# Making the output product's first 1024 columns in pairs of row blocks by pairs of column blocks, two of them with seven products

## The chip, the cores and the metric

The kernel runs on one core of one Trainium2 chip. The metric is the time of one execution on the device, in microseconds (us); smaller is better. Three executions of the kernel before took 1020.9, 1021.13 and 1021.59 us, so the median is 1021.13 us. PE is TensorE (matrix multiplication), DVE is VectorE, ACT is ScalarE, POOL is GpSimd and SP is SyncE, which here only issues transfers.

## The reference, cut to what matters

The input is one sequence of 256 rows with 2048 features. After a normalisation and one wide projection, two mixers (attention and a short gated convolution) make `y_mla` and `y_conv`. They are merged by gates, the merged rows go through one more 2048 by 2048 product, and the result is normalised and added to the input:

```
merged = jax.nn.sigmoid(g_mla) * y_mla + jax.nn.sigmoid(g_conv) * y_conv
out = jnp.einsum('bsd,de->bse', merged, w_out)
x = x + _rmsnorm(out, post_norm_g)
```

The change concerns `out`, that is `merged` (256 x 2048) times `w_out` (2048 x 2048), and what stands around it in the program.

## The kernel before

**Numbers in two parts.** Every operand of a product is a float32 array that is written as a sum of two arrays of TensorE's faster format, a high part and a low part. ACT copies an array to its high part, and DVE takes the difference as its low part (`split_act`, lines L287 and L288). One logical product is then three matmuls: high by high, high by low, low by high (`product`; all matmuls have line L90). One matmul has a 128 x 128 stationary operand (a piece of the activations, turned so that features lie on partitions) and 512 moving columns (a piece of a weight matrix).

**Weight units.** Weights come from HBM in units of 128 x 2048 numbers, 1 MB each, in the fixed order of the list `plan`. `take(i)` is called where unit i is used. It first calls `ahead(i)`, which issues the transfers of the units up to i + 2 (from SP, into one of three `raw` buffers) and the split of unit i + 1. A plain unit is split as two halves of 1024 columns, each into a buffer of the ring `whi` (high) and one of the ring `wlo` (low). Both rings have five buffers, so a new half waits until the buffer freed longest ago has been read by its last matmul. A `raw` buffer comes free when the last split that reads it is done. A scheduler then sets the order of instructions on each engine, but keeps matmuls in the order of the code; each engine runs its own list strictly in order.

**Seven products.** The four 2048 x 2048 products ahead of the output product are made in blocks of two row blocks by two column blocks: a weight unit holds, for one pair of k blocks, four 128 x 512 weight blocks. A plain pair takes 8 products (24 matmuls). Some pairs are done with seven products (21 matmuls), as in Winograd's form of Strassen's scheme: DVE makes four sums of weight blocks (`split_seven`, L229: `ts`), all of which are split as well (`th`, `tl`; the third block goes to `ph`, `pl`), and four differences of activation blocks (`mixed`, L670: `xm`, split into a `mix` tile). The seven results lie in seven PSUM banks, and DVE combines them at the block's end (`first_sums`, L1078). In these products all partial products of a kind are summed over the pairs in PSUM.

**The output product.** Its weights `wo` are 16 units: four column blocks of 512 by four groups of four k blocks. The list `out_order` (L158) sets their order: column blocks 0, 1, 2 with the first two k groups each, then column blocks 0, 1, 2 with the other two, then column block 3 with all four. Every unit takes 24 matmuls, 12 for each of the two row blocks. Six PSUM banks collect column blocks 0 to 2. The activations are `merged`, in the tile `x_both`; `features(c)` splits four k blocks of it, which the last part of the product before brings back from HBM turned (`turned`, L370, L378 and L382). `features(2)` and `features(3)` stand in the code at the sixth unit.

**Around it.** After the sixth unit the pool `spool` (sums, gates) and the stacks below it are closed, and ACT's queue issues the loads of `gb` (the gain, 1 MB) and `xr` (the input rows, 2 MB) into memory that comes free there (L1198, L1199). As each of column blocks 0 to 2 ends, `out_block` takes its squares on ACT (L1204) and multiplies by `gb` on DVE (L1207). The splits of the last column block go to buffers of their own in the pools `op` and `op_w`. The end of the program scales, adds `xr` and stores.

## Time and profile before

| | |
|---|---|
| times of three executions | 1020.9, 1021.13, 1021.59 us |
| the profiled execution's own time | 1021.97 us |
| its span in the profile | 1020.2 us |
| mean granted TensorE clock | 0.999 |
| PE busy | 1013.9 us of the span |
| DVE busy | 812.7 us of the span |
| ACT busy | 564.0 us of the span |
| read from HBM | 215.66 MB |

The span runs from the first to the last instruction that the profiler saw; the execution's own time is 1.77 us longer. A row of a timeline gives the start in the span, the duration, the engine, the source line, the operation, its output and its inputs; "x2" stands for two such instructions in a row, and a bracket for the idle time ahead of it and what ended it. Instructions of one engine overlap a little, so that the next one starts before the duration of the one before has passed.

### The profile page before, as it was taken

The numbers are of one execution on the slowest core, as the hardware profiler recorded it, in microseconds if no ns is written. First come the engines' busy times: TensorE is split into PE (matmuls) and PEld (weight loads), VectorE is DVE, ScalarE is ACT, GpSimd is POOL, SyncE is SP. The second block draws the span as 40 slices with busy tenths as digits, with TensorE's granted clock in tenths as the row PEclk, the third lists the DMA queues.
The fourth block names the chain that finished last, engine by engine and source line by source line (L and its number), as shares of the span: only waits on it lengthen the run. The fifth ranks groups of instructions, "written<-read, shape, count | busy, mean of one in ns | idle before, by whom it ended". The sixth has DMA issues, their size and how long they took to land.

```text
span 1020.2 us, 12873 instructions
## 1 busy us (share of the span) xinstructions
PE 1013.9 (99%) x4621; PEld 844.2 (83%) x4621; DVE 812.7 (80%) x1174; ACT 564.0 (55%) x793; POOL 178.9 (18%) x344
## 2 busy tenths in 40 slices
PE   9999999999999999999999999999999999999997
PEld 7888888888888888888888888888888888888886
DVE  7578777777777777777878799899989979898572
ACT  7665655555556455455554556565766545363551
POOL 4640421113311213212132220000000000123000
PEclk9999999999999999999999999999999999999999
DMA  9774776567675767757676765555546546586852
GB/s 343 282 271 186 259 237 234 204 219 257 219 273 185 243 232 242 271 186 239 222 253 236 267 243 208 209 209 202 206 171 243 191 180 216 172 313 217 332 195 83
DMA packets 44528, 233.27 MB, mean 229 GB/s; under 512 B 7952, under 2 KB 10512, under 8 KB 21552
## 3 DMA queue, kind: packets, MB, share of 16 engines
q1 hardware_dynamic: 32400, 199.67, 54.8%
q0 software_dynamic: 11632, 29.48, 8.8%
q10 hardware_dynamic: 432, 3.29, 0.8%
q8 instruction: 36, 0.59, 0.2%
q14 instruction: 28, 0.23, 0.1%
HBM read 215.66 MB, written 12.58 MB: 224 GB/s over the span
## 4 chain that ended last, share of the span: by engine, by line
PE 95%; DMA 3%; ACT 1%; DVE 0%; issue 0%; SPq 0%; DVEq 0%; ACTq 0%
PE cv L90 34%; PE q L90 18%; PE p L90 9%; PE out L90 9%; PE z L90 6%; PE d L90 6%; PE vv L90 2%; PE kn L90 2%; PE qa L90 2%; PE qn L90 2%; PE ckv L90 2%; PE sc L90 1%; PE qr L90 1%; PE o L90 1%; DMA raw<-wz_dram 1%; DMA at_f<-far_qa 1%
## 5 line engine op out<-in xcount | busy, mean ns | idle before, releaser
L287 ACT ACTIVATE whi<-raw 128x1024 fp32r<-128x1024 f32 (+1 forms) x351 | 356.3, 1032 | 323.4 <-PE cv L90 109.4
L288 DVE TENSOR_TENSOR wlo<-raw,whi 128x1024 fp32r<-128x1024 f32 (+1 forms) x349 | 412.1, 1191 | 132.5 <-ACT whi L287 125.2
L90 PE MATMUL cv<-whi,x_both 128*128 128x512 f32 x1024 | 319.8, 389 | 0.0
L90 PEld LDWEIGHTS cv<-whi,x_both 128*128 128x128 f32 x1024 | 192.3, 188 | 39.5
L90 PE MATMUL cv<-wlo,x_both 128*128 128x512 f32 x512 | 199.6, 390 | 0.0
L90 PEld LDWEIGHTS cv<-wlo,x_both 128*128 128x128 f32 x512 | 96.1, 188 | 19.5 <-DVE wlo L288 0.2
L90 PE MATMUL q<-whi,x_both 128*128 128x512 f32 x296 | 97.1, 389 | 0.0
L90 PE MATMUL z<-whi,x_both 128*128 128x512 f32 x256 | 80.0, 389 | 0.0
L90 PE MATMUL out<-whi,x_both 128*128 128x512 f32 x256 | 78.9, 389 | 0.0
L378 POOL DMA_DIRECT2D far<-g x32 | 17.4, 551 | 312.7 <-DVE g L370 310.0
L378 POOL DMA_DIRECT2D far<-via x64 | 35.2, 556 | 180.7 <-DVE via L370 180.7
L90 PE MATMUL p<-whi,x_both 128*128 128x512 f32 x186 | 66.4, 390 | 0.0
L90 PEld LDWEIGHTS q<-whi,x_both 128*128 128x128 f32 x296 | 55.6, 188 | 11.5
L90 PE MATMUL q<-wlo,x_both 128*128 128x512 f32 x148 | 57.6, 389 | 0.0
L90 PEld LDWEIGHTS out<-whi,x_both 128*128 128x128 f32 x256 | 48.0, 188 | 9.9
L90 PEld LDWEIGHTS z<-whi,x_both 128*128 128x128 f32 x256 | 48.1, 188 | 9.9
L287 ACT ACTIVATE th<-ts 128x1024 fp32r<-128x1024 f32 x42 | 44.3, 1054 | 19.8 <-DVE ts L229 14.1
L288 DVE TENSOR_TENSOR tl<-ts,th 128x1024 fp32r<-128x1024 f32 x42 | 51.1, 1218 | 2.4 <-ACT th L287 2.3
L90 PE MATMUL d<-whi,x_both 128*128 128x512 f32 x148 | 51.6, 389 | 0.0
L90 PE MATMUL z<-wlo,x_both 128*128 128x512 f32 x128 | 49.8, 389 | 0.0
L90 PE MATMUL out<-wlo,x_both 128*128 128x512 f32 x128 | 49.8, 389 | 0.0
L90 PE MATMUL q<-th,mix 128*128 128x512 f32 x126 | 42.3, 390 | 0.0
(287 smaller groups left out, 1569.3 us busy)
## 6 DMA issues: line engine op xcount, KB each, us to landing
raw<-wcv_dram SPq DMA_DIRECT2D x64, 1024.0 KB, 5.6
raw<-wd_dram SPq DMA_DIRECT2D x64, 1024.0 KB, 4.8
raw<-wz_dram SPq DMA_DIRECT2D x16, 1024.0 KB, 4.9
raw<-wo_dram SPq DMA_DIRECT2D x16, 1024.0 KB, 5.5
raw<-wqk_dram SPq DMA_DIRECT2D x8, 1024.0 KB, 5.9
cw<-cwr_dram POOLq DMA_DIRECT2D x24, 256.0 KB, 6.4
raw<-wc_dram SPq DMA_DIRECT2D x4, 1024.0 KB, 10.4
raw<-wv_dram SPq DMA_DIRECT2D x4, 1024.0 KB, 5.1
```

Source lines behind the costliest of these rows:

```text
L90: return tc.keep_in_program_order(nc.tensor.matmul(*a, **kw))
L287: a = nc.scalar.activation(hi, src, AF.Copy)
L288: b = nc.vector.tensor_tensor(lo, src, hi.bitcast(F32), op=ALU.subtract)
L378: tc.keep_in_program_order(queue.dma_start(out=f[i], in_=m))
```

## The change

**Order and grouping.** Column blocks 0 and 1 are no longer made one by one. Their weights come as eight units of the pair form (`wp`, one unit for each pair of k blocks, with four 128 x 512 blocks), and four banks `pair00`, `pair01`, `pair10`, `pair11` collect row block t by column block j. The 16 units now stand in this order: pairs 0, 1, 2, 3; column block 2 with k groups 0 and 1; pairs 4, 5, 6, 7; column block 2 with k groups 2 and 3; column block 3 with its four k groups.

**Seven products.** Pairs 5 and 7 are done with seven products. Unlike in the earlier blocks, no seven banks are free: three of the seven results are added into the pair banks, and the other four (`p1`, `q6`, `q5`, `q7`) go through two banks, first `p1` and `q6`, then `q5` and `q7`, and are combined by ACT (one copy) and DVE (four operations) while the pair runs. The two pairs' sums are added, and at the end the four pair banks are added to them, in SBUF (`ev_out`, `more_out`).

**Mixed activations.** For each of the two pairs four differences of 128 x 128 blocks and a split are made on DVE and ACT, behind `features(2)` and behind `features(3)`, at the same sixth unit.

**What moves.** `gb` and `xr` are loaded right behind the last block of the product before, instead of after the sixth unit. `spool` is closed after pair 7, instead of after the sixth unit. The squares and the gain of all three column blocks stand behind column block 2's last k group.

The diff, cut to its core:

```diff
-    out_order = [(c, k) for c in range(3) for k in range(2)] + [(c, k) for c in range(3) for k in (2, 3)]
-    out_order += [(3, k) for k in range(4)]
-    u_out = {ck: add(wo[ck[0], ck[1]]) for ck in out_order}
+    out_fast = (5, 7)
+    u_pair, u_out = {}, {}
+    for k in range(PAIRS):
+        u_pair[k] = add(wp[k])
+        if k == PAIRS // 2 - 1:
+            u_out.update({(2, kk): add(wo[0, kk]) for kk in (0, 1)})
+    seven.update(u_pair[k] for k in out_fast)
+    u_out.update({(2, kk): add(wo[0, kk]) for kk in (2, 3)})
+    u_out.update({(3, kk): add(wo[1, kk]) for kk in range(4)})
...
+    def pair_products(k):
+        w = take(u_pair[k])
+        for (t, j), ps in pair_banks.items():
+            for i in range(2):
+                product(ps[:, :], m_part(2 * k + i, t), w(block_of[i, j], R), k == i == 0, t == j == i == 1 and k == PAIRS - 2)
...
+    def pair_by_seven(k, name, home):
...
+        p1, q6 = (bank(f"{n}_{name}") for n in ("p1", "q6"))
+        product(p1[:, :], m_part(2 * k, 0), w["b11"], True, True)
+        product(q6[:, :], part(2), w["t2"], True, True)
+        nc.scalar.activation(t_a, p1[:, :], AF.Copy)
+        nc.vector.tensor_tensor(t_b, q6[:, :], t_a, op=ALU.subtract)
+        product(pair_banks[0, 0][:, :], m_part(2 * k + 1, 0), w["b21"], False, last)
+        product(pair_banks[0, 1][:, :], part(3), w["b22"], False, last)
+        product(pair_banks[1, 0][:, :], m_part(2 * k + 1, 1), w["t4"], False, last)
+        q5, q7 = (bank(f"{n}_{name}") for n in ("q5", "q7"))
+        product(q5[:, :], part(1), w["t1"], True, True)
+        product(q7[:, :], part(0), w["t3"], True, True)
+        nc.vector.tensor_tensor(o21, q7[:, :], t_b, op=ALU.add)
+        nc.vector.tensor_tensor(t_b, q5[:, :], t_b, op=ALU.add)
+        nc.vector.tensor_tensor(o22, q5[:, :], o21, op=ALU.add)
...
+        if kk:
             for j in (2, 3):
                 features(j)
-        out_products(pss[c], w, kk)
+                k = out_fast[j - 2]
+                mixed_turned(mix_m[k], lambda c, t: gate[0][t][:, c * R : (c + 1) * R], k)
+        out_products(pss[2], w, kk)
...
+            for a, b in zip(held, home):
+                nc.vector.tensor_tensor(a[:, :], a[:, :], b[:, :], op=ALU.add)
...
+    for tj, o in pair_out.items():
+        nc.vector.tensor_tensor(o, pair_banks[tj][:, :], o, op=ALU.subtract if tj == (1, 0) else ALU.add)
     spool.close()
```

**How the engines' lists move.** In the rows below the number behind `whi`, `wlo`, `raw`, `th`, `tl`, `ph`, `pl` and `ts` is that of the weight unit: before, 183 to 186 are column blocks 0, 0, 1 and 1 (k groups 2, 3, 2 and 3); now 183 to 186 are pairs 4, 5, 6 and 7, 187 and 188 are column block 2's k groups 2 and 3, and 189 to 192 are column block 3. The eighth unit of the stage is 184 in both.

The first place is PE's list at the eighth unit. Before, its first rows are these, where every matmul has a piece of `merged` as its stationary operand:

```order
L90 MATMUL out0_0_8330<-whi184_0_8565,x_both_101 128x512
L90 MATMUL out0_0_8330<-wlo184_0_8566,x_both_101 128x512
L90 MATMUL out0_0_8330<-whi184_0_8565,x_both_101 128x512 x2
L90 MATMUL out0_0_8330<-wlo184_0_8566,x_both_101 128x512
L90 MATMUL out0_0_8330<-whi184_0_8565,x_both_101 128x512
L90 MATMUL out0_0_8330<-whi184_1024_8569,x_both_101 128x512
```

The same place of the changed kernel, the beginning of pair 5 (`mix0_102` is the tile of mixed activations of this pair, both its parts):

```order
L90 MATMUL p1_a_8630<-whi184_8575,x_both_101 128x512
L90 MATMUL p1_a_8630<-wlo184_8576,x_both_101 128x512
L90 MATMUL p1_a_8630<-whi184_8575,x_both_101 128x512
L90 MATMUL q6_a_8631<-th184_1_8582,mix0_102 128x512
L90 MATMUL q6_a_8631<-tl184_1_8584,mix0_102 128x512
L90 MATMUL q6_a_8631<-th184_1_8582,mix0_102 128x512
L90 MATMUL pair00_8339<-ph184_8577,x_both_101 128x512
```

The fourth matmul of the unit now needs the high part of `mix0`, and the sixth its low part.

The second place is ACT's list ahead of and in the eighth unit. Before:

```order
L287 ACTIVATE whi184_1024_8569<-raw184_8506 128x1024
L1198 DMA gb_8560<-post_g_dram 128x2048
L1199 DMA xr_8558<-x_dram 128x4096
L287 ACTIVATE whi185_0_8599<-raw185_8563 128x1024
L287 ACTIVATE whi185_1024_8603<-raw185_8563 128x1024
L287 ACTIVATE whi186_0_8639<-raw186_8597 128x1024
```

The same place now:

```order
L293 ACTIVATE whi185_0_8622<-raw185_8573 128x1024
L293 ACTIVATE whi185_1024_8626<-raw185_8573 128x1024
L293 ACTIVATE ph186_8664<-raw186_8620 128x512
L293 ACTIVATE whi186_8662<-raw186_8620 128x1024
L293 ACTIVATE whi187_0_8711<-raw187_8660 128x1024
L1218 ACTIVATE ev_out_8571<-p1_a_8630 128x512
L293 ACTIVATE mix0_102<-xm21_8529 128x512
L293 ACTIVATE x_both_101<-g0_0_5616 128x4x128
```

The high part of `mix0` stands behind the high parts of units 186 and 187 and behind the copy of `p1`, and the two loads no longer stand here.

The third place is DVE's list at the same time. Before:

```order
L288 TENSOR_TENSOR wlo184_1024_8570<-raw184_8506,whi184_1024_8569 128x1024
L288 TENSOR_TENSOR wlo185_0_8600<-raw185_8563,whi185_0_8599 128x1024
L288 TENSOR_TENSOR wlo185_1024_8604<-raw185_8563,whi185_1024_8603 128x1024
L288 TENSOR_TENSOR wlo186_0_8640<-raw186_8597,whi186_0_8639 128x1024
L1207 TENSOR_TENSOR og_8559<-out0_0_8330,gb_8560 128x512
```

Now:

```order
L294 TENSOR_TENSOR pl186_8665<-raw186_8620,ph186_8664 128x512
L676 TENSOR_TENSOR xm21_8529<-g0_0_5616,xm21_8529 128x128
L235 TENSOR_TENSOR ts186_1_8667<-ts186_0_8666,raw186_8620 128x512
L294 TENSOR_TENSOR wlo186_8663<-raw186_8620,whi186_8662 128x1024
L294 TENSOR_TENSOR wlo187_0_8712<-raw187_8660,whi187_0_8711 128x1024
L235 TENSOR_TENSOR ts186_1_8667<-ts186_1_8667,raw186_8620 128x512
L294 TENSOR_TENSOR mix0_102<-xm21_8529,mix0_102 128x512
L294 TENSOR_TENSOR x_both_101<-g0_0_5616,x_both_101 128x4x128
L294 TENSOR_TENSOR x_both_101<-g0_1_5617,x_both_101 128x4x128
L676 TENSOR_TENSOR xm31_8540<-g0_1_5617,g0_0_5616 128x128
L676 TENSOR_TENSOR xm31_8540<-g0_1_5617 128x128
L1219 TENSOR_TENSOR ev_out_8571<-q6_a_8631,ev_out_8571 128x512
```

The low part of `mix0` (seventh row) now stands behind the splits of pair 7 and of the first half of unit 187, which before had nothing like them at this place.

More of the change, by code (lines that the diff above doesn't have):

```diff
@@ L84, in tile_layer @@
 @with_exitstack
-def tile_layer(ctx: ExitStack, tc: tile.TileContext, xw, w0, xb, x, pos, pvec, post_g, wc, wz, wcv, wkr, wqk, wqr, wv, cwr, wd, wo, out):
+def tile_layer(ctx: ExitStack, tc: tile.TileContext, xw, w0, xb, x, pos, pvec, post_g, wc, wz, wcv, wkr, wqk, wqr, wv, cwr, wd, wp, wo, out):
     nc = tc.nc
@@ L1044, in mixed_turned @@
         c, k = divmod(k, 2)
-        rows = [by_rows(src[:, c, t, :], 4) for t in range(NT)]
+        rows = [by_rows(src(c, t), 4) for t in range(NT)]
         mixed(dst, [[x[:, 2 * k + j] for x in rows] for j in range(2)], const.tile([P, HALF], F32, name=f"xm{c}{k}", tag="low", bufs=1)[:, : 4 * P])
@@ L1135, in between @@
                 split_group(at_place, at_t, 3)
-            mixed_turned(mix_at[fast[2, 0][i - 1]], at_t, fast[2, 0][i - 1])
+            mixed_turned(mix_at[fast[2, 0][i - 1]], lambda c, t: at_t[:, c, t, :], fast[2, 0][i - 1])
         elif (c, i) == (0, 3):
@@ L1154, in between @@
         if c == 0 and i in (1, 2):
-            mixed_turned(mix_cv[fast[3, 0][i - 1]], cv_t, fast[3, 0][i - 1])
+            mixed_turned(mix_cv[fast[3, 0][i - 1]], lambda c, t: cv_t[:, c, t, :], fast[3, 0][i - 1])
         elif c and i in (4, 5):
@@ L1170, in tile_layer @@
             come(m)
+    cv_stack.close()
+    cstack.close()
+    ends = ctx.enter_context(tc.tile_pool(name="ends", bufs=1, side="right"))
+    xr = ends.tile([P, NT, D], F32, name="xr")
+    gb = ends.tile([P, D], F32, name="gb")
+    nc.scalar.dma_start(out=gb[:, :], in_=post_g.to_broadcast([P, D]))
+    nc.scalar.dma_start(out=xr[:, :, :], in_=x)
     def out_product(ps, t, w, kk):
@@ L1179, in out_products @@
             out_product(pss[t], t, w, kk)
-    pss = [[bank(f"out0_{t}", tag=tag, bufs=1) for t, tag in enumerate(("st", "o"))]]
-    pss += [[bank(f"out1_{t}", tag="cv", bufs=2) for t in range(NT)], [bank(f"out2_{t}") for t in range(NT)]]
-    for i, (c, kk) in enumerate(out_order[:6]):
-        w = take(u_out[c, kk])
-        if i == 5:
+    pair_banks = {
+        tj: bank(f"pair{tj[0]}{tj[1]}", tag=tag, bufs=2 if tag == "cv" else 1)
+        for tj, tag in zip(quarters_of, ("st", "o", "cv", "cv"))
+    }
@@ new lines, in tile_layer @@
+    block_of = {(0, 0): 0, (1, 1): 1, (1, 0): 2, (0, 1): 3}
+    def pair_products(k):
[3 more added lines that the diff above has]
+                product(ps[:, :], m_part(2 * k + i, t), w(block_of[i, j], R), k == i == 0, t == j == i == 1 and k == PAIRS - 2)
+    mix_m = dict(zip(out_fast, (mix[k] for k in FAST)))
+    def pair_by_seven(k, name, home):
+        w = take(u_pair[k])
+        part = lambda j: tuple(mix_m[k][:, o, j * P : (j + 1) * P] for o in range(2))
+        last = k == out_fast[-1]
+        ev, more = home
+        t_a, t_b, o21, o22 = (e[:, o : o + R] for e in (ev, more) for o in (0, R))
+        p1, q6 = (bank(f"{n}_{name}") for n in ("p1", "q6"))
[12 more added lines that the diff above has]
+        nc.vector.tensor_tensor(o22, q5[:, :], o21, op=ALU.add)
@@ L1186, in tile_layer @@
+    for k in range(PAIRS // 2):
+        pair_products(k)
+    pss = {2: [bank(f"out2_{t}") for t in range(NT)]}
+    for kk in (0, 1):
+        w = take(u_out[2, kk])
+        if kk:
             for j in (2, 3):
                 features(j)
-        out_products(pss[c], w, kk)
+                k = out_fast[j - 2]
+                mixed_turned(mix_m[k], lambda c, t: gate[0][t][:, c * R : (c + 1) * R], k)
+        out_products(pss[2], w, kk)
+    held = [
+        hp.tile([P, HALF], F32, name="ev_out", tag="qa1", bufs=1),
+        const.tile([P, HALF], F32, name="more_out", tag="low", bufs=1),
+    ]
@@ new lines, in tile_layer @@
+    for k in range(PAIRS // 2, PAIRS):
+        if k == out_fast[0]:
+            pair_by_seven(k, "a", held)
+        elif k in out_fast:
+            home = [sums(f"held{i}") for i in range(2)]
+            pair_by_seven(k, "b", home)
+            for a, b in zip(held, home):
+                nc.vector.tensor_tensor(a[:, :], a[:, :], b[:, :], op=ALU.add)
+        else:
+            pair_products(k)
+    pair_out = dict(zip(quarters_of, (e[:, o : o + R] for e in held for o in (0, R))))
+    for tj, o in pair_out.items():
+        nc.vector.tensor_tensor(o, pair_banks[tj][:, :], o, op=ALU.subtract if tj == (1, 0) else ALU.add)
@@ L1189, in tile_layer @@
     spool.close()
-    cv_stack.close()
-    cstack.close()
     op_w = ctx.enter_context(tc.tile_pool(name="op_w", bufs=1, side="right"))
     op = ctx.enter_context(tc.tile_pool(name="op", bufs=1))
-    xr = op.tile([P, NT, D], F32, name="xr")
     og = op.tile([P, NT, D], F32, name="og")
-    gb = op.tile([P, D], F32, name="gb")
-    nc.scalar.dma_start(out=gb[:, :], in_=post_g.to_broadcast([P, D]))
-    nc.scalar.dma_start(out=xr[:, :, :], in_=x)
     def out_block(c, t, ps):
@@ L1264, in finish_by_two @@
         store(t, 1024, 1280, o[:, 512:])
-    for c in range(3):
-        for kk in (2, 3):
-            out_products(pss[c], take(u_out[c, kk]), kk)
-        for t in range(NT):
-            out_block(c, t, pss[c][t])
+    for kk in (2, 3):
+        out_products(pss[2], take(u_out[2, kk]), kk)
+    for (t, c), o in pair_out.items():
+        out_block(c, t, o)
+    for t in range(NT):
+        out_block(2, t, pss[2][t])
     nc.vector.reduce_sum(part[:, :], ssq[:, :, :3], axis=mybir.AxisListType.X)
@@ L1359 @@
         "wd": np.stack([in_pairs(w) for w in (g_m, g_c, w_o_mla, w_o_conv)]),
-        "wo": w_out.reshape(4, 4, P, 4, 512).transpose(3, 0, 2, 1, 4).reshape(4, 4, P, UNIT),
+        "wp": in_pairs(w_out)[0],
+        "wo": w_out.reshape(4, 4, P, 4, 512).transpose(3, 0, 2, 1, 4).reshape(4, 4, P, UNIT)[2:],
     }
```

## The prediction, made before the changed kernel ran

> **What bounds the kernel now.** I read the page first, then what PE waited for, then the chain that ended last, then the output product in stretches.

> ```profile
> span 1020.2 us, 12873 instructions
> ...
> PE 1013.9 (99%) x4621; PEld 844.2 (83%) x4621; DVE 812.7 (80%) x1174; ACT 564.0 (55%) x793; POOL 178.9 (18%) x344
> ...
> PE 95%; DMA 3%; ACT 1%; DVE 0%; issue 0%; SPq 0%; DVEq 0%; ACTq 0%
> ```
> ```profile
> PE idle L90 <- PEq L1363: 0.8, 1, 0.8
> PE fin L90 <- ACT dg L1251: 0.4, 1, 0.4
> PE vv L90 <- DVE f L446: 0.3, 1, 0.3
> ```
> ```profile
> 925.16 87.05 PE out L90 x384
> ```
> ```profile
> 925.00:947.00 22.00, 22.00 (x99) 18.22 (x98) 16.79 (x22) 9.01 (x10) 10.93 (x20) 1.00 0.74 256
> 947.00:968.00 21.00, 21.00 (x94) 17.41 (x93) 12.59 (x13) 10.81 (x14) 0.00 (x0) 1.00 0.83 324
> 968.00:990.00 22.00, 22.00 (x98) 18.22 (x98) 15.52 (x15) 13.93 (x20) 0.00 (x0) 1.00 0.67 248
> ```

> PE is busy for 99% of the span, it waited three times for 1.5 us in all, and 95% of the chain is PE. The output product is one unbroken piece of that chain: 384 matmuls in 87.05 us, 0.2267 us each. So a matmul fewer is worth 0.2267 us, and every wait of PE that is added counts in full. The rows by stretch (behind the length stand PE's two busy times, then DVE's, ACT's and POOL's; the third number from the end is the granted clock) show what is left to hide new work: 8.4 of 21 us of DVE between 947 and 968.

> **What is removed.** Columns 0 to 1023 took 8 units of 24 matmuls, 192. Now six pairs take 24 and two take 21, 186. Six fewer: 6 x 0.2267 = **1.36 us gained**. No other matmul goes.

> **What is added, and where it lies.** I follow the engines' lists with durations of before.

> ```profile
> 925.00 0.39 PE L90 MATMUL out<-whi,x_both 128*128 128x512 f32 x1
> 941.09 0.61 PE L90 MATMUL out<-whi,x_both 128*128 128x512 f32 x2
> ```
> ```profile
> 914.32 2.01 ACT L287 ACTIVATE whi<-raw 128x1024 fp32r<-128x1024 f32 x2 [0.45 <-PE d L90]
> 916.23 0.57 ACT L1087 ACTIVATE ev<-p 128x512 f32<-128x512 f32 x1
> 941.51 1.06 ACT L287 ACTIVATE whi<-raw 128x1024 fp32r<-128x1024 f32 x1 [0.30 <-PE out L90]
> ```
> ```profile
> 740.66 1.21 DVE L288 TENSOR_TENSOR tl<-ts,th 128x1024 fp32r<-128x1024 f32 x1
> 741.80 0.48 DVE L670 TENSOR_TENSOR xm<-at_f 128x128 f32<-128x128 f32 x2
> 742.20 0.68 DVE L229 TENSOR_TENSOR ts<-ts,raw 128x512 f32<-128x512 f32 x1
> 742.80 1.21 DVE L288 TENSOR_TENSOR wlo<-raw,whi 128x1024 fp32r<-128x1024 f32 x1
> ...
> 946.69 2.59 DVE L288 TENSOR_TENSOR wlo<-raw,whi 128x1024 fp32r<-128x1024 f32 x2 [2.85 <-ACT whi L287]
> ```
> ```profile
> L178 SPq DMA_DIRECT2D raw<-wo_dram x1: 327/327/327, 942.5 to 942.5; - x1
> ...
> DMA to landing us min/median/max: 5.7/5.7/5.7
> ```

> Matmul n of the product starts at 925.00 + 0.2267 n, as long as nothing stops it. A buffer is free 0.42 us after its last matmul starts (the third unit's last at 941.09, ACT at 941.51). ACT's copy of 1024 columns takes 0.95 us where another follows (2.01 for two), of 512 columns 0.57. DVE starts an operation on 1024 columns 1.14 us after the one before (740.66, 741.80), on 512 after 0.60 (742.20, 742.80), on 128 after 0.20.

> A plain unit costs DVE 2 x 1.14 = 2.3 us. A unit with seven products costs four of 1024 columns and three of 512 (sums, splits) and four of 512 behind the products: 4 x 1.14 + 7 x 0.60 = 8.8 us, 6.5 more. Twice that, two sums of 1024, four last additions, and two mixtures (four of 128 columns and one of 512 each) make 13.0 + 2.3 + 2.4 + 2.8 = **20.5 us more DVE work**, most of it wanted before pair 7 ends. It does not fit beside PE everywhere. The first place where PE needs it is pair 5, behind 168 matmuls: `q6` wants `mix0` high at matmul 171 (963.77) and low at matmul 173 (964.22).

> - *When DVE can begin.* Unit 184's `raw` buffer is that of unit 181, free when unit 181's second half is split. That half waits for the matmul 68 (940.41 + 0.42 = 940.8), ACT is done at 941.9 and DVE at 943.1. The transfer lands 5.7 us later (the row of 942.5): 948.8. Unit 182 keeps DVE until 948.5, so the wait for the transfer hardly counts.
> - *What stands ahead.* From unit 184's first sum to `mix0` low DVE's list has 11 operations on 1024 columns, 9 on 512 and 4 on 128: 12.5 + 5.4 + 0.8 = 18.7, with the last one's end 18.8. The end is **967.6**, 3.4 us behind 964.2.
> - *ACT is not later.* `whi186` gets its buffer after matmul 164 (962.18 + 0.42 = 962.60), `whi187` follows until 964.5, the copy of `p1` until 965.1, `mix0` high until 965.7.

> So PE waits for `mix0` in two pieces, 1.9 us for the high part and the rest for the low part: **3.4 us lost**. Behind it PE and DVE run together: until DVE has read pair 5's `q5` for the last time its list has seven operations on 512 columns, three on 1024 and four on 128, 8.4 us, and some 1.1 us in which it waits for ACT's copies: 977.2. Pair 7's `q6`, which takes that bank, is due at 977.4 (matmul 216, 973.97, and the 3.4). In the same way DVE's step between `q6` and `q7` of pair 7 ends at 980.3, and `q7` is due at 980.8. No further wait, with 0.2 us to spare.

> *The bounds of that wait.* Below: if DVE had nothing in front, ACT's own list still gives `mix0` high at 965.7 and the low part 0.68 later, 966.4: 2.2 us. Above: if DVE's operations did not overlap, the 24 would take 11 x 1.21 + 9 x 0.68 + 4 x 0.28 = 20.6 us, and PE would wait 5.2. I take 3.4, since the rows from 740.66 on are such a list, and in them nothing takes the whole duration. [...]

> **What I cost at nothing.** `gb` and `xr` now go out at about 910 and share the engines with the units 178 and 179.

> ```profile
> L178 SPq DMA_DIRECT2D raw<-wo_dram x1: 328/328/328, 958.8 to 958.8; - x1
> ...
> DMA to landing us min/median/max: 11.1/11.1/11.1
> ```
> ```profile
> L178 SPq DMA_DIRECT2D raw<-wo_dram x2: 327/328/328, 911.2 to 912.3; - x2
> ```
> ```profile
> 927.36 1.22 DVE L288 TENSOR_TENSOR wlo<-raw,whi 128x1024 fp32r<-128x1024 f32 x1
> ```

> Before, a unit issued beside them took 11.1 us to land. At 911.2 that gives 922.3. DVE was at that unit's second half at 927.36, is there at about the same time now, and PE comes to the unit at 930.4, so some 4 us cover it, and only what goes beyond would cost. On ACT `gb` stands behind a copy of 1.06 us; its memory is free three matmuls (0.7 us) after the copy's buffer, so ACT doesn't stand still for it. The transposed activations, the last block's sums and SP's and POOL's lists keep their places. The four last additions and the later `out_block`s run beside column block 3, where DVE was busy for a third of the time:

> ```profile
> 990.00:1012.20 22.20, 22.20 (x99) 18.38 (x99) 6.92 (x12) 3.91 (x8) 0.00 (x0) 1.00 0.13 48
> ```
> ```profile
> DMA to landing us min/median/max: 4.7/5.8/6.9
> ```

> The tightest there is the very last unit: its `raw` buffer is that of unit 189, which DVE splits behind pair 7's combination, about 10.7 us after pair 7's last product (981.7 with the 3.4), so at 992.4. It lands in 4.7 at best (the last row, of the two units issued at 981.0 and 982.1), so at 997.1, and DVE, in the order of its list, has the halves at 1000.1 and 1001.3, for matmuls due at 1000.8 and 1002.1. That holds by some 0.7 us. The end behind the last matmul is unchanged.

> **The sum**, against the profiled execution's own 1021.97 us: -1.36 + 3.4 = +2.0, 1024.0. That execution was 0.84 above the median of 1021.13, so in those terms **1023.2 us**, 0.2% slower, which is also about what a measurement of this kernel can tell from no change (0.2% is 2.04 us, so the bounds are 1019.1 and 1023.2).

> **The rivals.**

> - *No wait: the mixture is in time* (0.10). PE gets `mix0` by 964.2 if DVE reaches it 3.4 us earlier, that is if the 18.8 us began by 945.2. For it: DVE sat idle for 2.85 us ahead of each pair of splits at 946.69. Against: those gaps lie ahead of 948, when unit 184 isn't there. Time: 1021.13 - 1.36 = 1019.8, not slower.
> - *ACT alone sets it* (0.08): DVE takes less than the sum, PE waits 2.2 us. 1021.13 + 0.8 = 1022.0.
> - *A second wait* (0.18): the 0.2 us at pair 7 or the 0.7 us at the last unit do not hold; each is lost by one operation of 1024 columns, 1.14 us. 1023.2 + 1.1 = 1024.3. For it: three places with less than 0.8 us to spare; against: a longer first wait gives DVE time at the later places.
> - *DVE's operations don't overlap* (0.05): 5.2 instead of 3.4, 1025.0.
> - *The clock falls* (0.04): a PE that stands still might go on at half pace for as long as it stood, 3.4 us in which 1.7 us of work is done, so +1.7: 1024.9. Against: the granted clock is 1.00 in each of the rows above, and the wait is cut by two matmuls. [...]
> - *The change doesn't save what it says*: PE's list has the 378 matmuls that the diff gives, so none.

> **How the numbers follow.** The forecast has 0.55, from 1022.2 to 1024.2, about half of it on each side of the 0.2%. Slower by over 0.2%: 0.28 + 0.18 + 0.05 + 0.04 = 0.55. Within: 0.27 + 0.08 + 0.08 = 0.43. Faster: 0.02, from the no-wait case. The range takes in both bounds of the wait (1021.13 - 1.36 + 2.2 = 1022.0 and + 5.2 = 1025.0) with the spread of the runs around them, 1021.3 to 1025.3, and leaves out mainly the no-wait case, 0.10.

> **What would show it.** In the profile of the changed kernel: 378 matmuls of the output product at 0.2267; in what PE waited for, `q` for ACT `mix` by about 1.9 us and for DVE `mix` by about 1.5, once each, near 964 to 968; DVE without a gap from 948.8 to about 977; no wait at pair 7 or at the last column block. I am wrong if DVE is idle shortly ahead of `mix0`, if PE waits at `p1` or `q7` as well, or if the first units wait for DMA.

## The result and the profile after

| | before | after |
|---|---|---|
| median of six executions each | 1021.36 us (1020.9 to 1021.65) | **1028.34 us** (1028.12 to 1028.65) |
| span of the profiled execution | 1020.2 us | 1026.9 us |
| mean granted TensorE clock | 0.999 | 0.997 |

The ratio is 1.0069, with a 95% interval from 1.0058 to 1.0079: the change makes the kernel 0.7% slower. Forecast were 1023.2 us and a range up to 1025.3.

The page's busy times, and the last part of the chain that ended last (start, length, work):

```profile
span 1026.9 us, 12911 instructions
...
PE 1015.6 (99%) x4615; PEld 845.4 (82%) x4615; DVE 831.6 (81%) x1208; ACT 569.1 (55%) x801; POOL 179.0 (17%) x344
```
```profile
924.52 15.65 PE pair L90 x69
942.54 7.86 DMA raw<-wp_dram
970.07 3.84 PE pair L90 x9
976.05 5.44 PE pair L90 x24
986.25 32.66 PE out L90 x144
```

PE is still "busy" for 99%, which hides a third of the loss, since PE at half pace counts as busy (3.41 of the 3.41 us from 972.00 to 975.41, at a granted clock of 0.50). The chain tells more: the output product is no longer one piece of PE, but is broken by a transfer at 942.54, and nine matmuls at 970 take 3.84 us where 24 at 976 take 5.44.

What PE waited for in the changed kernel (in all, times, longest):

```profile
PE q_a L90 <- ACT mix L293: 4.2, 1, 4.2
PE q_a L90 <- DVE mix L294: 0.9, 1, 0.9
```

PE's timeline at that place (start, duration, operation; the bracket is the idle time ahead of it):

```profile
963.10 0.39 PE L90 MATMUL p_a<-whi,x_both 128*128 128x512 f32 x1
967.64 0.50 PE L90 MATMUL q_a<-th,mix 128*128 128x512 f32 x1 [4.15 <-ACT mix L293]
967.98 0.40 PE L90 MATMUL q_a<-tl,mix 128*128 128x512 f32 x1
969.28 0.80 PE L90 MATMUL q_a<-th,mix 128*128 128x512 f32 x1 [0.90 <-DVE mix L294]
969.87 0.63 PE L90 MATMUL pair<-ph,x_both 128*128 128x512 f32 x1
970.30 0.63 PE L90 MATMUL pair<-pl,x_both 128*128 128x512 f32 x1
...
975.89 0.39 PE L90 MATMUL pair<-whi,x_both 128*128 128x512 f32 x1
```

The same stretches as before (length; PE, its weight loads, DVE, ACT, POOL busy; granted clock, DMA share, GB/s):

```profile
925.00:947.00 22.00, 22.00 (x98) 18.21 (x98) 16.49 (x20) 8.29 (x9) 10.83 (x20) 1.00 0.74 247
947.00:968.00 21.00, 16.85 (x74) 13.36 (x72) 18.53 (x24) 12.40 (x16) 0.08 (x1) 1.00 0.67 244
968.00:990.00 22.00, 21.10 (x81) 16.87 (x80) 16.73 (x25) 6.93 (x9) 0.00 (x0) 0.84 0.41 144
990.00:1012.20 22.20, 22.20 (x100) 18.38 (x99) 18.21 (x27) 13.68 (x24) 0.00 (x0) 1.00 0.15 50
```

Two losses stand next to each other. First PE waits for `mix0`, the mixture of pair 5, in two pieces. Between the third `p1` matmul (963.10) and the last of `q6` (969.28) lie 6.18 us, where three steps of 0.2267 would be 0.68: **5.5 us lost**. Then PE is busy, but at half pace: the 16 matmuls from 969.28 to 975.89 take 6.61 us instead of 3.63, 0.43 apart at a granted clock of 0.50. That is **3.0 us more**. With 0.2 us in pair 4, where PE waited a little for the split features, the stage loses 8.7 us and gains 1.36. It began 0.6 us earlier than in the profile of before (its first matmul starts at 924.36 instead of 925.00; in the profiles of all the runs below it starts between 923.96 and 924.82); 8.7 - 1.36 - 0.6 is the 6.7 us between the two spans.

DVE in front of `mix0` (the first and the last of its operations), the transfer of unit 184, and ACT's list ahead of the high part:

```profile
950.42 1.23 DVE L235 TENSOR_TENSOR ts<-raw 128x1024 f32<-128x1024 f32 x1 [2.47 <-DMA raw<-wp_dram]
968.54 0.68 DVE L294 TENSOR_TENSOR mix<-xm,mix 128x512 fp32r<-128x512 f32 x1
```
```profile
L184 SPq DMA_DIRECT2D raw<-wp_dram x1: 328/328/328, 942.5 to 942.5; - x1
...
DMA to landing us min/median/max: 7.9/7.9/7.9
```
```profile
962.23 1.06 ACT L293 ACTIVATE whi<-raw 128x1024 fp32r<-128x1024 f32 x1 [0.21 <-PE pair L90]
965.53 1.06 ACT L293 ACTIVATE whi<-raw 128x1024 fp32r<-128x1024 f32 x1 [2.24 <-DMA raw<-wo_dram]
966.49 0.58 ACT L1218 ACTIVATE ev_out<-p_a 128x512 f32<-128x512 f32 x1
966.97 0.62 ACT L293 ACTIVATE mix<-xm 128x512 fp32r<-128x512 f32 x1
```

DVE works without a gap from 950.42 to 969.22, 18.8 us. It begins late because unit 184 took 7.9 us to land. The high part of `mix0` is late because ACT, in the order of its list, first waits 2.24 us for unit 187's transfer.

### The profile page after: what moved, and what is told of

Same layout as the page of the kernel before. It is cut to its first block, busy times and chain, and to the rows that moved or that the text cites. A ratio compares the mean times of both kernels' runs of the same rounds, so it can differ in the third digit from the quotient of the medians.

```text
span 1026.9 us, 12911 instructions
## 1 busy us (share of the span) xinstructions
PE 1015.6 (99%) x4615; PEld 845.4 (82%) x4615; DVE 831.6 (81%) x1208; ACT 569.1 (55%) x801; POOL 179.0 (17%) x344
## 4 chain that ended last, share of the span: by engine, by line
PE 96%; DVE 2%; DMA 1%; issue 0%; ACT 0%
PE cv L90 34%; PE q L90 18%; PE p L90 8%; PE z L90 8%; PE d L90 6%; PE out L90 3%; PE pair L90 3%; PE qa L90 2%; PE kn L90 2%; PE qn L90 2%; PE vv L90 2%; PE ckv L90 2%; PE sc L90 1%; PE qr L90 1%; PE o L90 1%; DVE wlo L294 1%
## 5 line engine op out<-in xcount | busy, mean ns | idle before, releaser
L90 PE MATMUL cv<-whi,x_both 128*128 128x512 f32 x1024 | 319.8, 389 | 0.0
L90 PEld LDWEIGHTS cv<-whi,x_both 128*128 128x128 f32 x1024 | 192.3, 188 | 39.5
L90 PE MATMUL cv<-wlo,x_both 128*128 128x512 f32 x512 | 199.5, 390 | 0.0
L90 PEld LDWEIGHTS cv<-wlo,x_both 128*128 128x128 f32 x512 | 96.1, 188 | 19.3
L90 PE MATMUL q<-whi,x_both 128*128 128x512 f32 x296 | 97.1, 389 | 0.0
L90 PE MATMUL z<-whi,x_both 128*128 128x512 f32 x256 | 79.9, 389 | 0.0
L90 PE MATMUL p<-whi,x_both 128*128 128x512 f32 x186 | 66.4, 390 | 0.0
L90 PEld LDWEIGHTS q<-whi,x_both 128*128 128x128 f32 x296 | 55.5, 188 | 11.6
L293 ACT ACTIVATE th<-ts 128x1024 fp32r<-128x1024 f32 x46 | 48.5, 1054 | 22.1 <-DVE ts L235 16.1
L294 DVE TENSOR_TENSOR tl<-ts,th 128x1024 fp32r<-128x1024 f32 x46 | 56.0, 1218 | 2.7 <-ACT th L293 2.5
L90 PE MATMUL q<-wlo,x_both 128*128 128x512 f32 x148 | 57.6, 389 | 0.0
L90 PEld LDWEIGHTS z<-whi,x_both 128*128 128x128 f32 x256 | 48.1, 188 | 9.8
L90 PE MATMUL d<-whi,x_both 128*128 128x512 f32 x148 | 51.6, 389 | 0.0
L90 PE MATMUL z<-wlo,x_both 128*128 128x512 f32 x128 | 49.8, 389 | 0.0
L90 PE MATMUL q<-th,mix 128*128 128x512 f32 x126 | 42.3, 390 | 0.0
L90 PEld LDWEIGHTS p<-whi,x_both 128*128 128x128 f32 x186 | 34.9, 188 | 7.3
L384 POOL DMA_DIRECT2D far<-cw x48 | 26.1, 551 | 79.6 <-DVE cw L376 77.7
L90 PE MATMUL out<-whi,x_both 128*128 128x512 f32 x128 | 39.7, 389 | 0.0
## 6 DMA issues: line engine op xcount, KB each, us to landing
raw<-wcv_dram SPq DMA_DIRECT2D x64, 1024.0 KB, 5.8
raw<-wd_dram SPq DMA_DIRECT2D x64, 1024.0 KB, 5.0
raw<-wz_dram SPq DMA_DIRECT2D x16, 1024.0 KB, 4.9
raw<-wqk_dram SPq DMA_DIRECT2D x8, 1024.0 KB, 5.7
raw<-wp_dram SPq DMA_DIRECT2D x8, 1024.0 KB, 7.9
raw<-wo_dram SPq DMA_DIRECT2D x8, 1024.0 KB, 4.8
raw<-wc_dram SPq DMA_DIRECT2D x4, 1024.0 KB, 10.5
```

The lines of the kernel that those rows point to most:

```text
L90: return tc.keep_in_program_order(nc.tensor.matmul(*a, **kw))
L293: a = nc.scalar.activation(hi, src, AF.Copy)
L294: b = nc.vector.tensor_tensor(lo, src, hi.bitcast(F32), op=ALU.subtract)
L384: tc.keep_in_program_order(queue.dma_start(out=f[i], in_=m))
```

## The experiments

The theories: **A**, PE stands still because `mix0` is due too early, and the standstill then halves the clock. **B**, the grouping and the two early loads cost by themselves (**B2**: the early loads). **C**, DVE has more work in this stretch than the stretch has room for, so a wait that is moved turns up elsewhere. **D**, pairs with seven products cannot pay here. **E**, the clock fell for another reason. The diffs are cut to their core, and "..." stands for lines left out. The medians of the kernel before beside the three groups of runs were 1021.4, 1021.43 and 1021.32 us; ratios are to it, with 95% intervals.

**The grouping alone.**

```diff
-    out_fast = (5, 7)
+    out_fast = ()
```

> The changed kernel with all eight pairs made by eight products: the grouping, the order of units, the early loads and the late end of spool stay, the two times seven products with their mixtures, sums and combinations go. The product again takes 384 matmuls. Theory A and theory C: no wait, 1021.4 less the 0.4 us by which the stage began earlier in the changed kernel's profile, 1020.9 to 1021.5. Theory B: still some us slower than before, 1023 or more.

Measured: 1021.46 us, ratio 0.9999 (0.9989 to 1.0008); PE waited nowhere in the stage. B falls: order, weight units and early loads cost nothing. Unit 184 took 8.9 us to land here, and nobody waited for it.

**Extra matmuls in the first gap.**

```diff
+        for _ in range(14 if name == "a" else 0):
+            matmul(q6[:, :], m_part(2 * k, 0)[0], w["b11"][0], start=True, stop=True)
         product(q6[:, :], part(2), w["t2"], True, True)
```

> The changed kernel with 14 extra matmuls in pair 5, between p1 and q6, into q6's own bank (their sums are thrown away). They need 3.2 us and lie inside the standstill of 4.15 us, which leaves gaps of about 1 us. Theory A (PE stands still for mix0 for some 5.2 us in two pieces, and that standstill then halves the granted clock, which costs another 3.3 us): granted clock 1.00 from 968 to 976, time 1028.3 - 3.3 = 1025.0, and 1024.7 to 1026 if DVE is now late for pair 7. Theory B (the loss lies in the new grouping, the wp units and the two early loads): 1028.3. Theory C (DVE's work sets the pace to the end of pair 7; the slow clock only fills time in which PE would wait for DVE anyway): 1027.5 to 1028.5, with a new wait of PE at pair 7.

Measured: 1026.44 us, 1024.74 to 1032.98 in six executions, ratio 1.0059 (1.0036 to 1.0081). In the profiled one the clock was 1.00 throughout, and DVE was 1.1 us later than in the changed kernel, so a second gap of 2.1 us stayed open. The mean clock of the slowest execution was 0.996, of the others 0.998 to 1.000. The direction is A's, and the new wait at pair 7 that C expected did not come in that profile; the scatter left the size open.

**Extra matmuls in both gaps.**

```diff
+            for _ in range(14):
+                matmul(q6[:, :], m_part(2 * k, 0)[0], w["b11"][0], start=True, stop=True)
...
+            matmul(q6[:, :], ah, bh, start=True, stop=False)
+            matmul(q6[:, :], ah, bl, start=False, stop=False)
...
+            for _ in range(6):
+                matmul(q5[:, :], m_part(2 * k, 0)[0], w["b11"][0], start=True, stop=True)
+            matmul(q6[:, :], al, bh, start=False, stop=True)
```

> The changed kernel with extra matmuls in both gaps of pair 5: 14 into q6's bank ahead of q6's first matmul, and 6 into q5's bank between q6's second and third (their sums are thrown away). PE then stands still for at most about 1 us at a time. Theory A (of the 8.5 us that PE loses, about 5.3 are the wait for mix0 and about 3.1 the halved clock): the wait stays, the clock is 1.00 in every run, 1028.3 - 3.1 = 1025.2 less nothing else, and the runs lie closer together than with the fillers in the first gap alone, where the second of 2.1 us stayed open. Theory C (DVE sets the end of pair 7 whatever the clock does): 1027 to 1028.5 with a new wait at pair 7.

Measured: 1025.88 us (1024.49 to 1026.21), ratio 1.0041 (1.0025 to 1.0056), mean clock 0.999 or 1.000 in every execution, no wait at pair 7. So useless work made the kernel 2.5 us faster than the changed one. That is 0.6 less than expected, in a range of executions of 1.7 us.

**What makes the clock fall.** Seven standstills were put into the kernel before.

```diff
+        matmul(stand_ps[:, :], m_part(0, 0)[0], w(0, 512)[0], start=True, stop=True)
...
+        nc.vector.tensor_tensor(st, stand_ps[:, :], other, op=ALU.subtract)
+        for _ in range(n):
+            nc.vector.tensor_tensor(st, st, other, op=ALU.subtract)
...
+        matmul(stand_ps[:, :S], ident[:, :], stand[:, :S], start=True, stop=True)
```

> The kernel before with seven added standstills of PE in the output product: behind a unit's last matmul an extra matmul into a spare bank, a chain of DVE operations on its result (3, 4, 5, 6, 7, 4 and 9 operations, 0.60 us each), and an extra matmul that needs the chain's result (the extra results are thrown away). That makes standstills of some 2.2, 2.8, 3.4, 4.0, 4.6, 2.8 and 5.8 us, longer where other operations of DVE stand in the chain, with 11 us of matmuls between them. Theory A (a standstill of about 4 us halves the granted clock for some 6.8 us): granted clock 1.00 behind those below 3.4, 0.5 for 6.8 us behind those of 4 us and more, each of these costing 3.4 us more than its own length; time about 1021.4 + 26 + 10 to 14. Theory E (the clock fell in the changed kernel for another reason, such as the work on DVE and ACT): 1.00 behind all of them, 1021.4 + 26.

Measured: 1080.83 us in one execution. DVE's other operations stood in the chains, so the standstills became 2.96 to 8.6 us, 39.5 in all. The clock was halved behind all seven (0.50 in the window that follows), also behind the shortest, so A's limit of about 4 us was wrong, and E falls. What the rows showed instead is a beat: in this run each fall and each recovery lies, to 0.1 us, at a multiple of 3.41 us from the others (the recovery at 1009.45 and the fall at 1043.58, for example, are 34.13 us apart, ten times 3.413; the first fall at 944.59 and the last recovery at 1067.47 are 122.88 us apart, 36 times that). So four kernels' stretches are cut along that beat: the changed kernel, then the run with the sevens later and the one with the sevens apart (both below), then this one. The first number behind the length is PE's busy time, the third from the end the clock.

```profile
961.76:965.17 3.41, 1.73 (x8) 1.11 (x6) 3.41 (x7) 1.32 (x2) 0.00 (x0) 1.00 0.67 226
965.17:968.59 3.42, 0.73 (x2) 0.30 (x2) 3.42 (x5) 3.06 (x5) 0.00 (x0) 1.00 0.61 254
968.59:972.00 3.41, 2.72 (x6) 2.16 (x7) 3.33 (x9) 0.05 (x2) 0.00 (x0) 0.50 0.66 219
972.00:975.41 3.41, 3.41 (x9) 2.65 (x8) 2.22 (x3) 2.74 (x3) 0.00 (x0) 0.50 0.23 94
```
```profile
989.24:992.65 3.41, 1.41 (x6) 1.17 (x7) 3.38 (x6) 0.00 (x0) 0.00 (x0) 0.99 0.00 0
992.65:996.07 3.42, 2.99 (x9) 1.79 (x7) 3.42 (x5) 1.12 (x2) 0.00 (x0) 0.51 0.00 0
```
```profile
1001.09:1004.50 3.41, 1.66 (x8) 1.07 (x7) 3.41 (x5) 3.41 (x12) 0.00 (x0) 1.00 0.00 0
```
```profile
1006.03:1009.45 3.42, 2.87 (x7) 2.31 (x8) 1.72 (x3) 2.00 (x2) 0.00 (x0) 0.50 0.82 326
...
1040.17:1043.58 3.41, 0.98 (x4) 0.86 (x5) 2.27 (x4) 0.00 (x0) 0.00 (x0) 1.00 0.00 0
1043.58:1046.99 3.41, 3.41 (x9) 2.67 (x8) 0.00 (x0) 0.00 (x0) 0.00 (x0) 0.50 0.00 0
```

A window in which PE was busy for 41% or less (1.41, 0.98, 0.73 of 3.41) was followed by one at half clock (0.50 or 0.51); one of 49% or 51% (1.66, 1.73) was not. At half clock, a window of 80% (2.72) was followed by another at half clock, and behind one of 84% (2.87) the clock was back at 1.00. No other window of the seven profiles in which the clock fell (these four and those of the runs with the mixtures on POOL, with the mixture ahead of the copy of `p1` and with the loads back), each cut along its own beat, says otherwise; what happens between these shares no run shows. So the changed kernel paid for two windows, of which PE was idle for 0.7: (6.83 - 0.7) / 2 = 3.1 us, beside 3.0 counted above. A standstill needn't be long: in the run with the sevens later one of 2.43 us was followed by a fall (0.51 from 992.65).

**The mixtures on another engine**, for the two mixtures of this stage and their low parts alike:

```diff
-        minus = lambda o, a, b: nc.vector.tensor_tensor(o, a, b, op=ALU.subtract)
+        minus = lambda o, a, b: eng.tensor_tensor(o, a, b, op=ALU.subtract)
...
+        eng.tensor_tensor(dst[:, 1, :], raw, dst[:, 0, :].bitcast(F32), op=ALU.subtract)
...
-                mixed_turned(mix_m[k], lambda c, t: gate[0][t][:, c * R : (c + 1) * R], k)
+                mixed_turned(mix_m[k], lambda c, t: gate[0][t][:, c * R : (c + 1) * R], k, nc.gpsimd)
```

> The changed kernel with the differences and the low part of both mixtures made by POOL, which has nothing else to do there, instead of DVE. In the order of the lists ACT's high part of mix0 then stands ahead of unit 187, and DVE's list loses 2.8 us for each mixture. Theory A: mix0 is there ahead of matmul 171 unless POOL needs more than about 2 us for 512 columns; no standstill, clock 1.00, 1021.4 - 1.4 - 0.4 = 1019.6, at most 1021. Theory B: 1023 or more, since nothing of the grouping changes. Theory C: DVE has 5.6 us less to do, so 1028.3 - 5.6 = 1022.7, with waits at q6 and q7 of both pairs.

Measured: 1030.54 us, ratio 1.0091 (1.0076 to 1.0106). `mix0` was in time, but PE waited 1.6 us for features, 1.8 for the copy of `p1` and 4.0 for DVE's first combination, and the clock fell again (0.51 and 0.50 from 972.42 to 979.25). None of the theories had this time; C had waits at such places, but 8 us less. DVE's and POOL's rows in that run:

```profile
960.88 2.32 DVE L294 TENSOR_TENSOR tl<-ts,th 128x1024 fp32r<-128x1024 f32 x1
```
```profile
960.30 1.81 POOL L682 TENSOR_TENSOR mix<-xm,mix 128x512 fp32r<-128x512 f32 x1 [4.51 <-ACT mix L681]
```

DVE's operation takes 2.32 us instead of 1.22: until POOL's ends at 962.11, and then 1.09 more, about its own time. Why it takes that long beside POOL's the rows do not show. So this run took no time off DVE, which began that first combination at 973.96 where the changed kernel has it at 970.75, and it can't tell A from C.

**The sevens later.** Numbers below 8 are pairs, 10 to 13 column block 2's k groups 0 to 3:

```diff
-    for k in range(PAIRS):
...
+    out_line = (4, 6, 12, 5, 13, 7)
+    for k in (0, 1, 2, 3, 10, 11) + out_line:
```

> The changed kernel with another order of the units: pairs 4 and 6, then column block 2's third k group, pair 5 (seven), column block 2's last k group, pair 7 (seven), column block 3. Pair 5's q6 is due at matmul 219 instead of 171, 10.9 us later; the work is the same (the two halves of the first unit of column block 3 go through the ring of five buffers). Theory A: mix0 is in time, clock 1.00, 1019.6 to 1020.2. Theory B: 1023 or more. Theory C: DVE has the same work in less time up to the last column block, so waits of some us behind pair 7 or in column block 3, 1022 to 1025.

Measured: 1029.86 us, ratio 1.0085 (1.0068 to 1.0102). PE no longer waited for `mix0`. It waited at column block 3 instead:

```profile
991.24 0.50 PE L90 MATMUL out<-whi,x_both 128*128 128x512 f32 x1 [2.43 <-DVE held L1227]
996.06 0.49 PE L90 MATMUL out<-whi,x_both 128*128 128x512 f32 x1 [0.43 <-ACT whi L294]
998.96 0.50 PE L90 MATMUL out<-wlo,x_both 128*128 128x512 f32 x1 [2.41 <-DVE wlo L295]
```

These 5.3 us and two falls of the clock (to 0.51 at 992.65 and at 999.48) are C's answer: the same work of DVE, now short of time behind pair 7. C had the place but not the time, 1022 to 1025, since it left out the clock.

**The sevens apart.**

```diff
-    for k in range(PAIRS):
...
+    out_line = (4, 6, 5, 12, 7, 13)
+    for k in (0, 1, 2, 3, 10, 11) + out_line:
```

> The changed kernel with the units behind the sixth in the order pair 4, pair 6, pair 5 (seven), column block 2's third k group, pair 7 (seven), column block 2's last k group, column block 3. Theory A (only mix0's due time counts; it is now matmul 195 instead of 171): 1021.45 - 1.36 = 1020.1. Theory C (DVE's work has to fit ahead of what comes next): mix0 in time and no wait at pair 7, which is due 5.4 us later than before; but behind pair 7 only 24 + 12 matmuls, 8.2 us, lie ahead of the second unit of column block 3, whose split came 10.3 us behind pair 7's last product in the run with the sevens later: a wait of about 2 us there, 1022.1, and 3.3 more if the clock falls.

Measured: 1035.56 us, ratio 1.0141 (1.0124 to 1.0158): a miss for both. Pair 6 needs `features(3)`, now one unit earlier, and in ACT's and DVE's lists those splits still stood behind `mix0`:

```profile
967.51 0.79 PE L90 MATMUL pair<-whi,x_both 128*128 128x512 f32 x1 [5.11 <-ACT x_both L294]
970.58 1.22 PE L90 MATMUL pair<-whi,x_both 128*128 128x512 f32 x2 [1.84 <-DVE x_both L295]
```

The order that I chose made a new wait of its own. The run says nothing on `mix0`; at the end it shows the forecast shortage at column block 3, 2.4 us in two waits.

**The mixture ahead of the copy of `p1`.**

```diff
-        if kk:
+        if not kk:
             for j in (2, 3):
                 features(j)
```

> The changed kernel with features(2), features(3) and the mixtures written at the fifth unit instead of the sixth. In the lists almost nothing moves but this: ACT makes the high part of mix0 ahead of the copy of p1, 0.5 us earlier. So the first standstill should be 3.65 instead of 4.15 us and the second 0.5 longer, the same in sum. Theory A with a limit near 4 us: the clock stays 1.00, 1028.3 - 3.3 = 1025.0. Theory A with a limit at 3.4 us: still halved, 1028.3. Theory C: as the changed kernel, 1027.5 to 1028.5.

Measured: 1028.02 us, ratio 1.0066 (1.0052 to 1.0079), standstill 4.6 us and 0.7, clock halved (0.50 from 968.18 to 975.00). The shorter standstill did not come about in the profiled execution, so it doesn't test a limit; its two waits are 5.3 us together (5.05 in the changed kernel).

**The loads back.**

```diff
-    nc.scalar.dma_start(out=gb[:, :], in_=post_g.to_broadcast([P, D]))
-    nc.scalar.dma_start(out=xr[:, :, :], in_=x)
...
+                if j == 2:
+                    tc.keep_in_program_order(nc.scalar.dma_start(out=gb[:, :], in_=post_g.to_broadcast([P, D])))
+                    tc.keep_in_program_order(nc.scalar.dma_start(out=xr[:, :, :], in_=x))
```

> The changed kernel with the loads of gb and xr issued from ACT's list behind the first splits of features(2), at about 956 as in the kernel before, instead of 909. Theory B2 (the early loads delay the transfers of the whole stage, unit 184's too, and with it mix0): unit 184 lands in 5.7 us instead of 7.9, the standstill is 2 us shorter, 1026.3 or, if the clock then holds, 1023. Theories A and C (the early loads cost nothing that counts): the first units land in 5 to 7 us instead of 10, which nobody waited for, unit 184 in about 8 as now, and units 186 and 187 share the engines with the 3 MB and land in 9 to 11 us, 3 to 6 later than now; ACT's high part of mix0 stands behind unit 187, so 1031 to 1035.

Measured: 1030.17 us, ratio 1.0088 (1.0075 to 1.0102). The first two units land in 4.8 and 7.5 us instead of 9.5 and 10.9, units 186 and 187 in 9.2 and 9.6. Unit 184:

```profile
L184 SPq DMA_DIRECT2D raw<-wp_dram x1: 328/328/328, 942.8 to 942.8; - x1
...
DMA to landing us min/median/max: 7.1/7.1/7.1
```

B2 falls: without the early loads unit 184 still took 7.1 us, and the kernel became slower, not faster, though not quite as slow as the 1031 to 1035 of A and C. Here the clock was at half for three windows (0.50, 0.50 and 0.51), from 965.8 to 976.0.

The new order needn't be the reason for the slow transfer either. The run with the standstills has the units and the loads of the kernel before, and there the eighth unit's transfer, issued behind the first standstill, took as long:

```profile
L178 SPq DMA_DIRECT2D raw<-wo_dram x1: 328/328/328, 943.6 to 943.6; - x1
...
DMA to landing us min/median/max: 7.0/7.0/7.0
```

**One pair with seven products.** Pair 7 alone, and then pair 5 alone:

```diff
-    out_fast = (5, 7)
+    out_fast = (7,)
```

> The changed kernel with pair 5 made plain, so that only pair 7 is done with seven products (381 matmuls, one mixture, no sum of two pairs' results). Theory A (PE stands still because mix0 is due too early): the mixture is due at matmul 195 and DVE has some 10 us less to do ahead of it, no wait, clock 1.00, 1021.45 of the eight plain pairs less 3 x 0.2267 = 1020.8. Theory C (from unit 184's landing at 950.4 to pair 7's q6 DVE has some 27.5 us of operations for the 23 us that PE leaves it, wherever the mixture stands): half of the addition fits, no wait, 1020.8 as well. Theory D (a pair with seven products costs PE more than it saves, by the turn of the banks p1, q6, q5, q7): waits in pair 7, 1021.5 to 1024.

Measured: 1020.44 us (1020.15 to 1021.2 in 11 executions), ratio 0.9992 (0.9983 to 1.0001), no wait in the stage, clock 1.00. The interval just takes in no change, so the times alone don't show a gain. The profile does: from the chain's beginning to the last weight matmul the stage takes 85.97 us (924.29 to 1010.26), where that of the eight plain pairs takes 86.65 (924.12 to 1010.77). Three matmuls fewer, 0.68 us, came through, and D falls for this pair.

```diff
-    out_fast = (5, 7)
+    out_fast = (5,)
```

> The changed kernel with pair 7 made plain, so that only pair 5 is done with seven products, at the place where PE stood still. Theory A (the mixture at this place is due too early): the same wait of some 5 us, 1021.45 - 0.7 + 5, so 1025 to 1029 with the clock. Theory C (what is too much is the sum of DVE's operations; ahead of mix0 in DVE's list those of pair 7's unit go): from unit 184's landing at 950.4 DVE has 8 operations on 1024 columns, 6 on 512 and 4 on 128 up to the low part of mix0, 13.5 us, so it is there at 964, which is when it is due: a wait of 0 to 0.8 us, no fall of the clock, 1020.8 to 1021.6.

Measured: 1023.95 us, ratio 1.0025 (1.0015 to 1.0036), clock 1.00.

```profile
963.98 0.50 PE L90 MATMUL q_a<-th,mix 128*128 128x512 f32 x1 [0.66 <-ACT mix L293]
...
968.97 0.50 PE L90 MATMUL q_a<-th,mix 128*128 128x512 f32 x1 [0.61 <-DVE ev_out L1219]
```

At the same place `mix0` is now late by 0.7 us instead of more than 5: with pair 7's operations out of DVE's list the wait went, as C says. C's time, at most 1021.6, was 2.4 us too low. In the profile PE loses 2.65 us in the stage, against the 0.68 that the pair saves: about 1.2 around `mix0`, and 1.3 where `q5` and `q7` take over the banks of `p1` and `q6`, behind ACT's copy (done at 967.34, `q5` starts at 967.40) and DVE's first combination (the second row). In the changed kernel PE did not wait at that turn. So at this place D is right for a single pair: it costs more than it saves.

**The sevens where DVE idles.**

```diff
-    out_fast = (5, 7)
+    out_fast = (3, 7)
-    for k in range(PAIRS):
...
+    out_line = (0, 1, 2, 10, 11, 3, 4, 5, 6, 7)
+    for k in out_line:
...
+    mixed_turned(mix_m[3], merged, 3)
...
+        if k == 4:
+            mixed_turned(mix_m[7], merged, 7, sums("xm31")[:, : 4 * P])
```

> Two pairs with seven products again, but pairs 3 and 7, in the order pairs 0, 1, 2, column block 2's first two k groups, pairs 3 to 7, the rest as in the changed kernel. The mixture of pair 3 needs nothing that comes back from HBM late, and lies in the stretch from 938 to 950 where DVE idled for some 8 us in the kernel before. Theory C (DVE's work must be spread over time in which it idles): no wait, or one below 1 us, clock 1.00, 1021.45 - 1.36 = 1020.1. Theory D (two pairs with seven products can't be had in this stage at all): waits of several us at pair 3's q6, at pair 4 for the features, or at pair 7, 1023 to 1030.

Measured: **1020.07 us** (1019.27 to 1020.66 in 11 executions), ratio 0.9986 (0.9977 to 0.9994). The same two pairs' worth of work: 378 matmuls, DVE busy for 832.9 us of the span (831.6 in the changed kernel), and no wait of PE in the stage, so D falls. Besides the pair and the order, the place of pair 7's mixture changed: it is written ahead of pair 4, with a buffer of its own. Its stretches:

```profile
925.00:947.00 22.00, 22.00 (x98) 18.21 (x98) 21.37 (x29) 10.60 (x12) 10.90 (x20) 1.00 0.78 263
947.00:968.00 21.00, 21.00 (x94) 17.38 (x93) 20.12 (x28) 12.65 (x17) 0.00 (x0) 1.00 0.65 239
968.00:990.00 22.00, 22.00 (x99) 18.22 (x98) 18.69 (x23) 12.18 (x20) 0.00 (x0) 1.00 0.43 154
```

DVE is busy for 21.4 of the first 22 us, where in the changed kernel it was for 16.5: 4.9 us of its work were moved to a place where nothing else wanted them. This version is faster than both kernels, than the kernel before by 0.14%. From its last weight matmul (1009.59) and that of the eight plain pairs (1010.77), with chains of the stage that begin at 924.30 and 924.12, the stage is shorter by 1.36 us, exactly the six matmuls.

## Why the prediction was wrong

- *Six matmuls fewer are worth 1.36 us*: right, shown by the last run's stage.
- *PE waits at pair 5's `q6` for `mix0`, and nowhere before*: right place, right engine, 0.2 us in pair 4 apart. *DVE's list in front of it takes 18.8 us*: measured 18.8.
- *The transfer lands 5.7 us later: 948.8*: **wrong, the first failed step.** I took the landing time from the kernel before, for the same place, and called the wait for it unimportant, since DVE seemed busy until 948.5. In the changed kernel it took 7.9 us, DVE idled for 2.47 us and began at 950.42, 1.6 us later than I had it. In the changed kernel and eight of the runs with pairs the eighth unit's transfer, issued between 942.1 and 943.1, took 7.1 to 8.9 us. With matmuls due 0.6 us earlier, since the stage began earlier, the 3.4 us became about 5.5. The upper bound of 5.2 for the wait stood for another reason (operations that don't overlap), and did not cover it. The range itself would have held a wait of 5.5 (1021.13 - 1.36 + 5.5 = 1025.3), but only at its very end and by luck. Why this transfer took longer stays open: the early loads are not the reason (B2), and the pair form of the weights is not either, at least not alone, since in the run with the sevens later a unit of column block 2, issued at 948.0, took 7.0 us, where its like took 4.8 before. It may not be the new order at all, since this transfer took 7.0 us in the run with the standstills too: the 5.7 of one profile may have been the low end of what this place gives.
- *ACT is not later; the wait comes in two pieces, 1.9 and 1.5*: wrong in size. The forecast gave unit 187's transfer no time, though that unit's high part stands ahead of `mix0` in ACT's list. ACT stood 2.24 us for it, so the first piece was 4.15. The sum was DVE's all the same.
- *The clock falls* (a rival at 0.04, 1.7 us): **the second failed step, and the larger one.** My reasons against it were that the granted clock was 1.00 in every row and that the wait was cut by two matmuls. The first was no evidence, since PE never stood still in those rows, and the second was wrong: two matmuls stood in the window ahead of the fall too (PE busy for 0.73 of its 3.42 us), and the clock fell all the same; in these runs it fell behind windows with 41% of work or less, whether or not a gap was unbroken. By that share, which is an estimate, even the 3.4 us of the forecast, with 0.45 us of matmuls between its pieces, could have left such a window. That half pace lasts as long as the standstill, from which the 1.7 us came, no run shows: here the clock was at 0.50 for two windows of 3.41 us. The first of them, with the second gap in it, had 80% of work, the second 100%. Measured 3.0 us.
- *No further wait, with 0.2 us to spare at pair 7 and 0.7 at the last unit*: right for the profiled execution, but helped by 5 us more of PE's time than I had given DVE. In the run with extra matmuls in both gaps there was none either, without the 3 us of the clock. How tight it is showed where the work was moved (the sevens later).
- *What I cost at nothing*: right. Eight plain pairs took 1021.46 us, and putting the loads back made it slower.

1024.0 was forecast for the profiled execution and 1028.65 measured, 4.7 more. About 2.1 of it are the wait, 3.0 the clock, 0.2 pair 4, less 0.6 of the earlier start. The cause behind both is C: some 19 us of additional DVE work (busy for 831.6 us instead of 812.7), put where the bounding engine leaves it no room. That it is the place and not the amount is shown by pairs 3 and 7.

## What to carry to other kernels

When a change trades the bounding engine's work for that of a helper, cut the profile into stretches and put the new work where the helper idles, ahead of its due time, before counting the gain. Take the time at which a transfer lands with a spread (the eighth unit's here took 5.7 to 8.9 us), not as one number from the same place of another order. And price the waits of TensorE with the clock behind them as well: in the profiles here each single wait of 2.41 us or more in the output product came with one to three windows of 3.41 us at a granted clock of 0.50 or 0.51; one of 2.1 us, with extra matmuls ahead of it, with none.
